# A hybrid decoder layer: the output projection as seven block products, its weights made ahead by jobs

## The chip, the cores and the metric

The kernel runs on one core of a Trainium2 chip. The time is the device time of one execution in microseconds, from three runs. The engines are TensorE (PE, matrix products), VectorE (DVE), ScalarE (ACT), GpSimd (POOL) and SyncE (SP), which here issues transfers. Transfers run on the core's 16 DMA engines.

## The reference

One layer on 1024 positions of width 1024, float32. What matters here:

```python
merged = (gates[:, :, 0] * (y_a @ w_branch_a[l])
          + gates[:, :, 1] * (y_b @ w_branch_b[l])
          + gates[:, :, 2] * (y_c @ w_branch_c[l]))
x = x + merged @ w_out[l]
x = x + 0.5 * swiglu(rmsnorm(x, ffn2_norm[l]), ffn2_w_gu[l], ffn2_w_down[l])
```

Ahead of it stand a first such FFN (`ffn1`, d_ff 2816) and the three branches a (spatial gating), b (latent attention) and c (memory attention). The change concerns the product of `y_b`, the gates' middle term, the product with `w_out`, and where their weights are prepared.

## The kernel before

**Arithmetic.** Float32 products are made of three: every operand is split into a high part (an ACT copy to a rounded type, tiles `whi`) and a low part (a DVE subtraction, `wlo`), `split` at L139 and L142 (or L146 and L147). `mm3` (L158 to L160) issues high x high, high x low and low x high into one PSUM bank, as 128x128 weights against 128x512 columns. Activations lie transposed: 8 tiles of 128 features, and two halves of 512 positions each.

**Fewer products in the FFNs.** The FFNs already multiply 2 x 2 blocks with seven products instead of eight. Their operands are sums of blocks named `b11`, `b12`, `b22`, `b21`, `t1` to `t4`: for activations made by `OpNorm` out of the normalised rows, for weights by `sums` (L1443) and stored or kept as splits.

**The first FFN's down** (`down`, from L2088) is a nest of seven loops, one for each product, with six steps each: five with 24 matmuls and one with 12. `fetch` (L2117) has SP load the quarter blocks of w_down (L2126, only in the first three loops) and a slice of the stored activations (`tdb..`, `tdt..`, L2128). `ahead()` calls it three steps ahead of use, and `prepare` (L2137) splits what came, one step ahead. Extra work hangs on steps (loop, step): `pre` in front of the matmuls, `post` behind them. There `gates.first(0)` (transfers of four blocks) stands at (1, 0), `gates.sums(0)` (four DVE sums, L1443) at (1, 4), and `norm.tokens(0)`, whose PE transposes are L410 and whose DVE reduction is L413, ahead of the matmuls of (5, 2). PE, SP, DVE and ACT run this in the order in which the code is written; a transfer that SP must wait for holds all behind it.

**The middle branch** (`branch_pairs(1, ...)`) takes 16 steps of 12 matmuls. DVE multiplies each with its gate (L573), GpSimd adds what the other two branches left in `mc` (L574), and the sum is split into `merged`.

**The projection** (`project`, L1146) runs over two halves and eight column tiles; each loads a 128x1024 tile of `w_out`, splits it, and makes 8 x 3 matmuls into a bank, which DVE adds to the rows of `x` (L1155), read back from `x1d`. `norm.feed` squares them on ACT and sums the squares on DVE (L1302, L1307). With half 0 done, the tasks `norm.first()` (sums and root, turn, part 0, part 1) are spread over the first four columns of half 1: DVE reduces (L413), takes the root (L192, then from L169 to L185), PE broadcasts (L425), DVE multiplies (L1344) and makes blocks (L1367, L147). PE reaches the units of the second FFN, which use these blocks, behind half 1; behind the first nine matmuls there stand half 1's token sums (L394).

Three tiles `raw` of 512 KB (128x1024, one tag with three buffers) serve loads of weights that are to be split.

## Time and profile before

| what | before |
|---|---|
| time, median of 3 runs | 2162.37 us (2161.65 to 2163.86) |
| the profiled execution | 2163.03 us |
| its span, first to last instruction | 2161.3 us |
| mean granted TensorE clock | 0.999 |

The time is that of the whole execution, the span that of the instructions in the trace. In the rows of groups and of the timeline, an entry names line, engine, operation, output and inputs; "x8" is a count. In the rows of windows, busy microseconds stand for each engine with their counts, then the clock, the share of the DMA engines and GB/s. Rows of transfers give KB of one and the median time from issue to landing.

### The profile page before, as it was taken

What the parts mean: (1) busy time and instruction counts of PE and PEld (TensorE: products, weight loads), DVE (VectorE), ACT (ScalarE), POOL (GpSimd) and SP (SyncE); (2) the same over time, 40 slices, a digit from 0 to 9 for tenths busy, and PEclk for the clock granted to TensorE, in tenths of its full rate; (3) what the DMA queues carried; (4) which work ended last, traced back from release to release, by engine and by line L of the source; (5) the groups of instructions that cost most, each with busy time, mean ns of one, the idle gap of its engine ahead of it and who ended that gap; (6) DMA issues with size and microseconds to landing.
All of it is one profiled execution on the core that took longest, in us unless ns stands there. A gap on an engine that the chain in (4) does not pass through costs nothing.

```text
span 2161.3 us, 27448 instructions
## 1 busy us (share of the span) xinstructions
PE 2151.9 (100%) x10112; PEld 1797.8 (83%) x10112; DVE 1572.1 (73%) x2371; ACT 910.3 (42%) x1486; POOL 255.0 (12%) x256
## 2 busy tenths in 40 slices
PE   9999999999999999999999999999999999999999
PEld 6888888888887888888988889988888888888887
DVE  7966666679889657655786679886876666657884
ACT  6433333243455434433555378833433223224332
POOL 0011111100000000000123311240011212110000
PEclk9999999999999999999999999999999999999999
DMA  4264555385332445641587832293133332347443
GB/s 148 92 220 159 190 180 175 119 318 193 118 124 94 147 164 180 223 149 61 212 283 259 314 105 69 75 348 104 40 127 103 110 97 100 103 144 288 169 129 104
DMA packets 137175, 342.56 MB, mean 158 GB/s; under 512 B 21713, under 2 KB 30033, under 8 KB 137041
## 3 DMA queue, kind: packets, MB, share of 16 engines
q1 hardware_dynamic: 136896, 340.81, 45.9%
q8 instruction: 79, 1.29, 0.2%
q14 instruction: 56, 0.45, 0.1%
q10 hardware_dynamic: 144, 0.00, 0.0%
HBM read 230.90 MB, written 109.86 MB: 158 GB/s over the span
## 4 chain that ended last, share of the span: by engine, by line
PE 91%; DVE 6%; ACT 1%; DMA 1%; issue 1%; SPq 0%; POOL 0%; ACTq 0%; DVEq 0%; POOLq 0%
PE one L158 15%; PE one L159 15%; PE one L160 15%; PE bank L158 13%; PE bank L159 13%; PE bank L160 13%; PE mm L158 1%; PE mm L159 1%; PE mm L160 1%; PE bank L1019 1%; PE one L1967 1%; DVE w L147 1%; DVE wlo L147 1%; DVE pr L997 1%; DVE wlo L142 1%
## 5 line engine op out<-in xcount | busy, mean ns | idle before, releaser
L146 ACT CAST whi<-x 128x1024 fp32r<-128x1024 f32 x202 | 192.3, 955 | 414.4 <-DVE x L1443 170.4
L147 DVE TENSOR_TENSOR wlo<-x,whi 128x1024 fp32r<-128x1024 f32 x202 | 241.2, 1195 | 58.9 <-ACT whi L146 19.6
L1471 DVE TENSOR_TENSOR t<-t,one 128x512 f32<-128x512 f32 x188 | 128.9, 686 | 190.8 <-PE one L160 190.7
L158 PE MATMUL bank<-h,whi 128*128 128x512 f32 x636 | 247.9, 390 | 0.0
L160 PE MATMUL bank<-h,wlo 128*128 128x512 f32 x636 | 247.5, 389 | 0.0
L159 PE MATMUL bank<-h,whi 128*128 128x512 f32 x636 | 247.5, 389 | 0.0
L158 PE MATMUL one<-h,whi 128*128 128x512 f32 x508 | 199.0, 392 | 0.0
L159 PE MATMUL one<-h,whi 128*128 128x512 f32 x508 | 198.4, 390 | 0.0
L160 PE MATMUL one<-h,wlo 128*128 128x512 f32 x508 | 198.3, 390 | 0.0
L158 PE MATMUL one<-w,whi 128*128 128x512 f32 x432 | 168.5, 390 | 0.0
L159 PE MATMUL one<-w,whi 128*128 128x512 f32 x432 | 168.1, 389 | 0.0
L160 PE MATMUL one<-w,wlo 128*128 128x512 f32 x432 | 168.1, 389 | 0.0
L142 DVE TENSOR_TENSOR wlo<-w,whi 128x1024 fp32r<-128x1024 f32 (+2 forms) x112 | 114.4, 1036 | 67.3 <-ACT whi L139 67.1
L139 ACT CAST whi<-w 128x1024 fp32r<-128x1024 f32 (+2 forms) x112 | 98.8, 901 | 149.8 <-PE one L159 55.6
L2067 POOL TENSOR_TENSOR raw<-raw 128x512 f32<-128x512 f32 x38 | 57.0, 1499 | 794.8 <-DVE raw L1908 684.8
L160 PEld LDWEIGHTS bank<-h,wlo 128*128 128x128 f32 x636 | 119.4, 188 | 24.9
L159 PEld LDWEIGHTS bank<-h,whi 128*128 128x128 f32 x636 | 119.4, 188 | 24.6
L158 PEld LDWEIGHTS bank<-h,whi 128*128 128x128 f32 x636 | 119.4, 188 | 24.4
L158 PE MATMUL bank<-whi 128*128 128x512 f32 x352 | 136.9, 389 | 0.0
L159 PE MATMUL bank<-wlo,whi 128*128 128x512 f32 x352 | 136.9, 389 | 0.0
L160 PE MATMUL bank<-whi,wlo 128*128 128x512 f32 x352 | 136.9, 389 | 0.0
L160 PEld LDWEIGHTS one<-h,wlo 128*128 128x128 f32 x508 | 95.8, 189 | 20.1
(406 smaller groups left out, 4892.2 us busy)
## 6 DMA issues: line engine op xcount, KB each, us to landing
x<-in_ffn_w_gu_dram SPq DMA_DIRECT2D x78, 512.0 KB, 5.1
w<-tdt SPq DMA_DIRECT2D x40, 512.0 KB, 4.2
gate<-raw SPq DMA_DIRECT2D x33, 512.0 KB, 3.0
tdb<-raw SPq DMA_DIRECT2D x64, 256.0 KB, 2.1
h<-in_ffn_w_down_dram SPq DMA_DIRECT2D x64, 256.0 KB, 6.0
w<-tdb SPq DMA_DIRECT2D x30, 512.0 KB, 5.1
tdt<-w SPq DMA_DIRECT2D x48, 256.0 KB, 2.4
x<-in_w_gate_dram SPq DMA_DIRECT2D x22, 512.0 KB, 5.9
```

The lines of the kernel that those rows point to most:

```text
L139: i = self.nc.scalar.copy(hi, src)
L142: return (eng or self.nc.vector).tensor_tensor(lo, src, hi.bitcast(F32), op=ALU.subtract)
L146: self.nc.scalar.copy(hi, src)
L147: return lambda: self.nc.vector.tensor_tensor(lo, src, hi.bitcast(F32), op=ALU.subtract)
L158: i = mmul(out, s[0], m[0], start=first, stop=False, **kw)
L159: mmul(out, s[0], m[1], start=False, stop=False, **kw)
L160: self.last = mmul(out, s[1], m[0], start=False, stop=last, **kw)
L997: nc.vector.tensor_tensor_reduce(out=pr[:, :m], in0=sc[:, :m], in1=self.mask[:, m0:m0 + m], scale=1.0, scalar=-NEG, op0=ALU.add, op1=ALU.m ...
L1019: nc.tensor.transpose(b[:, at:at + P], prs[t][:, kk * P:(kk + 1) * P], self.ident)
L1471: return self.nc.vector.tensor_tensor(out, x, y, op=ALU.add)
L1967: k.last = nc.tensor.matmul(b, w, norm.x(half, c), start=c == 0, stop=c == DT - 1)
L2067: sub = lambda d, x, y: (eng or nc.gpsimd).tensor_tensor(d, x, y, op=ALU.subtract)
```

## The change

The projection becomes seven products of 2 x 2 blocks, as in the FFNs (`merge`). Each has 4 column tiles x 4 row tiles x 3 matmuls. Its weights (`wo`, as high and low parts for each of seven products and two groups of columns) are made ahead: three of the fourteen by the existing jobs in `ffn1`'s up, eleven by `out_jobs` in `ffn1`'s down. Such a job loads 512 KB of `w_out` (or of a stored sum) into a `raw` tile, has GpSimd issue a transfer that adds a second block into it where two blocks make the sum (eight of eleven jobs), four steps later stores the sum where another job needs it (four of them), and a step after that splits the tile and stores both parts. Job i starts at step 4 + 7i // 4 of the 42, counted through the loops.

The middle branch is made in block order (b11, b12, b22, b21); in place of GpSimd's additions, eight transfers issued from GpSimd add `mc` into its tiles. DVE makes the sums of blocks and splits. The halves are swapped: what was half 0 of the rows is now half 1, in loads of `x1d` and in the stores. Norm and first weights of the second FFN are made within `merge`: the sum of squares is complete with the fifth product (for half 0), `norm.sums` stands at the second quarter of the sixth, `turn` and the first part behind its last, the second part behind the first quarter of the seventh. `gates.first` goes to step (4, 4) of the down loops, `gates.sums` to (5, 1). `layout` stores `w_out` as four quadrants.

The diff without the small parts (a bank argument of `turned_sums` and `norm_scale`, `store`'s columns, `layout`):

```diff
+        self.wo = self.dram.tile([7, 2, 2, P, D], F32, name="wo")
+        wo = [self.rounded(self.a["w_out"][g, i].unsqueeze(1), self.wo[n, g]) for n, i, g in ((0, 0, 0), (0, 0, 1), (6, 2, 0))]
         when = {}
-        for first, some in ((0, jobs), (1, small)):
+        for first, step, some in ((0, 2, jobs), (1, 2, small), (13, 2, wo[:2]), (16, 1, wo[2:])):
             for n, job in enumerate(some):
                 for f in range(2):
-                    at = when.setdefault(first + 2 * n + f, [])
+                    at = when.setdefault(first + step * n + f, [])
                     at.insert(0 if f else len(at), lambda job=job: next(job))
...
-        merged = [self.hrows() for _ in range(2)]
-        for _ in self.branch_pairs(
-                1, yb, mc, None, each, lambda d, f, x: self.split(*merged[f][d], x)):
-            pass
-        return merged
-
-    def project(self, merged, norm, sink):
...
+        return yb, mc
+    def out_jobs(self):
+        sums = self.dram.tile([3, 2, P, D], F32, name="wosum")
+        A11, A12, A22, A21 = range(4)
+        w, sync = self.a["w_out"], self.nc.sync
+        parts = {4: ((A11,), A21, 0), 1: (0, A22, 1), 3: (1, A12, None), 2: ((A21,), A22, None),
+                 0: ((A11,), None, None), 5: ((A12,), None, None), 6: ((A22,), None, None)}
+        def job(n, g):
+            x, (first, more, put) = self.raw(), parts[n]
+            sync.dma_start(x, sums[first, g] if isinstance(first, int) else w[g, first[0]])
+            if more is not None:
+                self.nc.gpsimd.dma_start(x, w[g, more], accum_op=ALU.add)
+            yield
+            if put is not None:
+                sync.dma_start(sums[put, g], x)
+            yield
+            hi, lo = self.wide("whi"), x.bitcast(F32R)
+            self.split(hi, lo, x)
+            for d, t in zip(self.wo[n, g], (hi, lo)):
+                sync.dma_start(d, t.bitcast(F32))
+            yield
+        order = [(n, g) for n in (4, 2, 1, 5, 3) for g in range(2)] + [(6, 1)]
+        when = {}
+        for i, j in enumerate(order):
+            j, q = job(*j), 4 + i * 7 // 4
+            for at, k in ((q, 2), (q + 4, 1), (q + 5, 0)):
+                when.setdefault(at, []).append((k, j))
+        return {(q // 6, q % 6): [lambda j=j: next(j) for _, j in sorted(x, key=lambda y: y[0])] for q, x in when.items()}
+    def merge(self, yb, mc, room, norm, load, early, later, sink):
+        nc, tt, h4 = self.nc, self.nc.vector.tensor_tensor, self.h4
+        names = ("b11", "b12", "b22", "b21")
+        raw = {n: [room() for _ in range(2)] for n in names}
+        w, op, x, banks = {}, {}, norm.x, {}
+        def put(name, p, src):
+            hi, lo = h4(F32R), h4(F32R)
+            op.setdefault(name, {})[p] = (hi, lo)
+            self.split(hi, lo, src)
+        def branch(name, k):
+            top, col = name[1] == "2", name[2] == "2"
+            dt, hf = 4 * top + k, int(col)
+            if dt not in w:
+                y = self.load(self.a["w_branch"][1, dt // 2])
+                w[dt], w[dt + 1] = y[:4], y[4:]
+            sig, d = self.row(), raw[name][k // 2]
+            nc.sync.dma_start(sig, self.sig[DT + dt][:, hf])
+            b = self.bank()
+            self.branch(b, w[dt], yb, hf)
+            tt(d[:, k % 2], sig, b, op=ALU.mult)
+            if k % 2:
+                nc.gpsimd.dma_start(d, mc[dt - 1:dt + 1, :, hf].rearrange("k p t -> p k t"), accum_op=ALU.add)
+        def weights(n):
+            out = []
+            for g in range(2):
+                ts = self.wide("whi"), self.wide("wlo")
+                for t, src in zip(ts, self.wo[n, g]):
+                    nc.sync.dma_start(t.bitcast(F32), src)
+                out += [tuple(t[:, u * 512:u * 512 + 512] for t in ts) for u in range(2)]
+            return out
+        def product(key, take, ws, name, first, last=True):
+            if first:
+                banks[key] = [None] * 4
+            for u in range(4):
+                if first:
+                    banks[key][u] = take()
+                for k in range(4):
+                    m = tuple(t[:, k % 2] for t in op[name][k // 2])
+                    s = tuple(t[:, k * P:(k + 1) * P] for t in ws[u])
+                    self.mm3(banks[key][u], s, m, first and k == 0, k == 3, skip_group_check=True)
+                yield u, banks[key][u]
+        def add(half, c, b, sign=ALU.add, parts=1):
+            y = x(half, c)
+            for n in self.parts(parts):
+                tt(y[:, n], y[:, n], b[:, n], op=sign)
+        for k in range(4):
+            branch("b11", k)
+            if k % 2:
+                put("b11", k // 2, raw["b11"][k // 2])
+        for k in range(4):
+            branch("b12", k)
+        ws = weights(0)
+        for k in range(4):
+            branch("b22", k)
+            if k % 2:
+                p = k // 2
+                b11, b12, b22 = (raw[n][p] for n in ("b11", "b12", "b22"))
+                tt(b12, b12, b22, op=ALU.subtract)
+                tt(b11, b12, b11, op=ALU.subtract)
+                put("t2", p, b11)
+        for k in range(4):
+            branch("b21", k)
+        load()
+        w2 = weights(1)
+        for u, b in product("a", self.single, ws, "b11", True):
+            add(1, 2 * u + 1, b, ALU.subtract)
+        p1 = banks["a"]
+        for p in range(2):
+            b11, b22 = raw["b11"][p], raw["b22"][p]
+            put("b22", p, b22)
+            nc.vector.scalar_tensor_tensor(b22, in0=b22, scalar=-1.0, in1=b11, op0=ALU.mult, op1=ALU.subtract)
+        for p in range(2):
+            put("t1", p, raw["b22"][p])
+        ws = weights(2)
+        for u, b in product("x", self.bank, w2, "t2", True):
+            add(1, 2 * u + 1, b, ALU.subtract)
+        for u in range(4):
+            add(0, 2 * u, p1[u])
+        for p in range(2):
+            put("t3", p, raw["b12"][p])
+        w2 = weights(3)
+        for u, b in product("x", None, ws, "t1", False):
+            add(0, 2 * u + 1, b, ALU.subtract)
+        for u in range(4):
+            add(0, 2 * u + 1, p1[u], ALU.subtract)
+        early()
+        for p in range(2):
+            put("b21", p, raw["b21"][p])
+            tt(raw["b21"][p], raw["b21"][p], raw["b11"][p], op=ALU.add)
+        ws = weights(4)
+        for u, b in product("x", None, w2, "b22", False):
+            add(0, 2 * u, b)
+            norm.feed(0, 2 * u)
+        for p in range(2):
+            put("t4", p, raw["b21"][p])
+        w2 = weights(5)
+        for u, b in product("y", self.bank, ws, "t3", True):
+            add(0, 2 * u + 1, b)
+            norm.feed(0, 2 * u + 1)
+            sink(0, 2 * u + 1)
+        ws = weights(6)
+        later()
+        norm.take = self.single
+        for u, b in product("a", None, w2, "b21", False):
+            add(1, 2 * u, b)
+            if u == 1:
+                with self.tc.high_priority(offset=600):
+                    norm.sums(0)
+            elif u == 3:
+                norm.turn(0)
+                norm.take = None
+                norm.part(0)
+            norm.feed(1, 2 * u)
+        for u, b in product("y", None, ws, "t4", False):
+            parts = 2 if u == 3 else 1
+            if u == 0:
+                norm.part(1)
+            add(1, 2 * u + 1, b, parts=parts)
+            norm.feed(1, 2 * u + 1, parts)
+            sink(1, 2 * u + 1)
 
...
-                    {(1, 0): [do(gates.first, 0)], (1, 4): [do(gates.sums, 0)],
+                    {(4, 4): [do(gates.first, 0)], (5, 1): [do(gates.sums, 0)],
...
-                    late)
+                    late, self.out_jobs())
...
-            merged = self.mixer(latents)
+            yb, mc = self.mixer(latents)
...
-            for half in range(2):
-                for p in range(DT // 2):
-                    nc.sync.dma_start(rows.take(half, p), x1d[half, p])
             norm = OpNorm(self, rows, lambda: self.g_ffn2)
             ffn = SwiGLU(self, a["ffn2_w_gu"], a["ffn2_w_down"], fp, norm, 2)
-            for f in range(2):
-                ffn.fetch(f, [ffn.w4] * 4)
-            self.project(merged, norm, lambda half, c: keep(x2d, norm.t, half, c))
+
+            def load():
+                for half, p in ((1, 0), (1, 1), (1, 2), (1, 3), (0, 0), (0, 1), (0, 2), (0, 3)):
+                    nc.sync.dma_start(rows.take(half, p), x1d[1 - half, p])
+
+            def early():
+                for f in range(2):
+                    ffn.fetch(f, [ffn.w4] * 4)
+
+            made = {}
+
+            def later():
+                for f in range(2):
+                    ffn.sums(f)
+                    made[f] = ffn.weights(f, "t")
+
+            with tc.manual_schedule(engines={mybir.EngineType.PE}):
+                self.merge(yb, mc, ffn.w4, norm, load, early, later, lambda half, c: keep(x2d, norm.t, half, c))
...
-                for act in [*acts[n, s], *post.get((n, s), ())]:
+                for act in [*acts[n, s], *post.get((n, s), ()), *jobs.get((n, s), ())]:
```

**SP in the first FFN's down.** Rows of SP while loop 1 (counted from 0) runs and slices for loop 2 (`tdt1_1`) are fetched. `in_ffn1_w_down_dram` is w_down, `in_x_dram` the residual input, a number behind a name tells tiles apart. Before:

```order
L2126 DMA w4_3663<-in_ffn1_w_down_dram 128x512
L2126 DMA w4_3665<-in_ffn1_w_down_dram 128x512
L2128 DMA w4_3949<-tdt1_1_99 128x1024
L1180 DMA x4_3951<-in_x_dram 128x2x512
L2126 DMA w4_3730<-in_ffn1_w_down_dram 128x512
L2126 DMA w4_3732<-in_ffn1_w_down_dram 128x512
L2128 DMA w4_3996<-tdt1_1_99 128x1024
L1180 DMA x4_3998<-in_x_dram 128x2x512
```

And now:

```order
L1154 DMA raw_3977<-wosum_3392 128x1024
L2281 DMA w4_3692<-in_ffn1_w_down_dram 128x512
L2281 DMA w4_3694<-in_ffn1_w_down_dram 128x512
L2283 DMA w4_3989<-tdt1_1_99 128x1024
L1323 DMA x4_3991<-in_x_dram 128x2x512
L1164 DMA wo_794<-whi_4031 128x1024
L1164 DMA wo_794<-raw_3799 128x1024
L1154 DMA raw_4036<-wosum_3392 128x1024
L2281 DMA w4_3753<-in_ffn1_w_down_dram 128x512
L2281 DMA w4_3755<-in_ffn1_w_down_dram 128x512
L2283 DMA w4_4044<-tdt1_1_99 128x1024
L1323 DMA x4_4046<-in_x_dram 128x2x512
```

Between the fetches there now stand the stores of a job's two parts (L1164) and, right behind them, the load of a later job (L1154) into one of the three `raw` tiles.

**DVE ahead of half 0's transposes in loop 5.** `L1307` of before and `L1462` now are the sums of squares, `L413` is the reduction behind the transposes (PE, L410 before). Before:

```order
L142 TENSOR_TENSOR wlo_4741<-h4_3640,whi_4740 128x512
L142 TENSOR_TENSOR wlo_4741<-w4_3642,whi_4740 128x512
L142 TENSOR_TENSOR wlo_4747<-w4_4647,whi_4746 128x1024
L2195 SCALAR_TENSOR_TENSOR x4_3925<-bank_4432,x4_3925 128x512
L1307 TENSOR_TENSOR t_4471<-t_4471,t_4711 128x512
L1307 TENSOR_TENSOR t_4471<-t_4471,t_4751 128x512
L413 TENSOR_REDUCE ts_4758<-bank_4759 128x4
```

And now:

```order
L142 TENSOR_TENSOR wlo_4855<-w4_4755,whi_4854 128x1024
L2350 SCALAR_TENSOR_TENSOR x4_3962<-bank_4524,x4_3962 128x512
L1462 TENSOR_TENSOR t_4563<-t_4563,t_4819 128x512
L1598 TENSOR_TENSOR x4_4752<-raw_4749,raw_4750 128x512
L1598 TENSOR_TENSOR raw_4751<-raw_4750,x4_4752 128x512
L1598 TENSOR_TENSOR x4_4752<-raw_4749,raw_4751 128x512
L1598 TENSOR_TENSOR raw_4751<-raw_4750 128x512
L1462 TENSOR_TENSOR t_4563<-t_4563,t_4859 128x512
L413 TENSOR_REDUCE ts_4870<-bank_4871 128x4
```

The four sums of `gates.sums` (L1598, L1443 of before) have moved between the last two sums of squares.

**DVE at the start of the second FFN.** From the last of the norm's multiplies (L1344 before, L1499 now) on. L147 with an `h4` output is the low part of a block for the units, first of `b22`, then of `t3`; L1367 (now L1522) makes `t3`, L1155 (now L1229) adds a bank to the rows. Before:

```order
L1344 SCALAR_TENSOR_TENSOR x4_12874<-x4_12874,c_ffn2_norm_3304,bank_13300 128x512 x2
L142 TENSOR_TENSOR wlo_13484<-raw_13481,whi_13483 128x512 x2
L1307 TENSOR_TENSOR t_13240<-t_13240,t_13296 128x512
L147 TENSOR_TENSOR h4_13348<-x4_12876,h4_13347 128x1024
L1367 TENSOR_TENSOR x4_12872<-x4_12876,x4_12872 128x1024
L1155 TENSOR_TENSOR x4_12882<-x4_12882,bank_13313 128x512
L1367 TENSOR_TENSOR x4_12874<-x4_12878,x4_12874 128x1024
L142 TENSOR_TENSOR wlo_13521<-raw_13518,whi_13520 128x512 x2
L1155 TENSOR_TENSOR x4_12882<-x4_12882,bank_13363 128x512
L147 TENSOR_TENSOR h4_13352<-x4_12872,h4_13351 128x1024
```

And now:

```order
L1499 SCALAR_TENSOR_TENSOR x4_12959<-x4_12959,c_ffn2_norm_3326,one_13472 128x512 x2
L147 TENSOR_TENSOR wlo_13599<-w4_13187,whi_13598 128x1024
L1462 TENSOR_TENSOR t_13405<-t_13405,t_13490 128x512
L147 TENSOR_TENSOR h4_13483<-x4_12961,h4_13482 128x1024
L1229 TENSOR_TENSOR x4_12949<-x4_12949,bank_13296 128x512
L1522 TENSOR_TENSOR x4_12957<-x4_12961,x4_12957 128x1024
L1229 TENSOR_TENSOR x4_12951<-x4_12951,bank_13314 128x512
L1522 TENSOR_TENSOR x4_12959<-x4_12963,x4_12959 128x1024
L1229 TENSOR_TENSOR x4_12953<-x4_12953,bank_13332 128x512
L1462 TENSOR_TENSOR t_13405<-t_13405,t_13519 128x512
L1229 TENSOR_TENSOR x4_12955<-x4_12955,bank_13350 128x256 x2
L147 TENSOR_TENSOR h4_13487<-x4_12957,h4_13486 128x1024
```

In both pieces the last row is the low part of `t3`'s first tiles. Between the multiplies and that row there now stand four additions of the seventh product's banks (the last in two parts) and two sums of squares, the splits of `w_out` (L142, `raw`) are gone.

38 lines of the change are left out of this document (11 added, 27 removed).

## The prediction

> **What bounds the kernel now.** First the page's rows of the span, of busy time and of the transfer rate by slice (a slice is 54 us), then three rows of the waits of TensorE (PE):
>
> ```profile
> span 2161.3 us, 27448 instructions
> PE 2151.9 (100%) x10112; PEld 1797.8 (83%) x10112; DVE 1572.1 (73%) x2371; ACT 910.3 (42%) x1486; POOL 255.0 (12%) x256
> GB/s 148 92 220 159 190 180 175 119 318 193 118 124 94 147 164 180 223 149 61 212 283 259 314 105 69 75 348 104 40 127 103 110 97 100 103 144 288 169 129 104
> ...
> PE bank L231 <- POOL ident masks.py:199: 1.5, 1, 1.5
> PE one L158 <- DVE raw L1471: 0.7, 2, 0.5
> PE bank L425 <- DVE rs_y L185: 0.7, 1, 0.7
> ```
>
> PE is one unbroken stream: its largest wait, for the identity matrix at the start, is 1.5 us, the next are under one. So two things change the time: matmuls added or taken away, and any new wait of PE. Work of the other engines, GpSimd (POOL) too, counts only where PE comes to wait for it. The profiled execution took 2163.0 us (1.7 lie outside its span), 0.7 over the median of 2162.37; I work from 2163.0.
>
> **The gain: matmuls.** PE's timeline, and the window of 80 us inside the old projection (PE busy and its count come first, DMA share and GB/s last):
>
> ```profile
> 1524.81 0.39 PE L158 MATMUL bank<-h,whi 128*128 128x512 f32 x1
> 1525.04 0.39 PE L159 MATMUL bank<-h,whi 128*128 128x512 f32 x1
> 1525.27 0.39 PE L160 MATMUL bank<-h,wlo 128*128 128x512 f32 x1
> ...
> 1445.00:1525.00 80.00, 80.00 (x358) 66.26 (x357) 51.01 (x81) 28.76 (x45) 0.00 (x0) 1.00 0.37 138
> ```
>
> A record lasts 0.39 us, yet the next one starts 0.23 later: records overlap, and the price of a matmul is the distance between starts. Eight of the 358 are transposes of 128 columns, some 0.7 us together, so a full one costs (80 - 0.7) / 350 = 0.2266 us. The old projection had 2 x 8 x 8 x 3 = 384, the seven products have 7 x 4 x 4 x 3 = 336, the middle branch keeps its 192. Saved: 48 x 0.2266 = **10.9 us** (with 0.39 it would be 18.7, too much). One product is 10.9 us as well, a quarter of it 2.72.
>
> **Cost 1: the start of the second FFN.** Rows of the timelines of VectorE (DVE) and PE there before:
>
> ```profile
> 1488.61 0.68 DVE L413 TENSOR_REDUCE ts<-bank 128x4 f32<-128x512 f32 x1
> ...
> 1490.41 0.16 DVE L192 TENSOR_SCALAR rms_v<-ts 128x4 f32<-128x4 f32 x1
> 1490.61 0.17 DVE L169 TENSOR_SCALAR rs_y<-rms_v 128x4 int32<-128x4 int32 x1
> ...
> 1494.54 5.35 DVE L1344 SCALAR_TENSOR_TENSOR x<-x,c_ffn_norm,bank 128x512 f32<-128x512 f32 x8
> 1499.80 1.29 DVE L142 TENSOR_TENSOR wlo<-raw,whi 128x512 fp32r<-128x512 f32 x2
> ...
> 1502.74 1.22 DVE L1367 TENSOR_TENSOR x<-x,x 128x1024 f32<-128x1024 f32 x1
> 1503.88 0.68 DVE L1155 TENSOR_TENSOR x<-x,bank 128x512 f32<-128x512 f32 x1
> 1504.48 1.22 DVE L1367 TENSOR_TENSOR x<-x,x 128x1024 f32<-128x1024 f32 x1
> ...
> 1521.61 0.69 DVE L1155 TENSOR_TENSOR x<-x,bank 128x512 f32<-128x512 f32 x1 [1.28 <-PE bank L160]
> ...
> 1526.85 0.39 PE L158 MATMUL one<-h,whi 128*128 128x512 f32 x1
> 1527.05 0.75 DVE L1155 TENSOR_TENSOR x<-x,bank 128x256 f32<-128x256 f32 x2 [3.31 <-PE bank L160]
> ...
> 1528.89 0.50 PE L394 MATMUL bank<-ones,t 128*128 128x1 f32 x4
> ```
>
> Prices from start to start: 0.60 us for 128x512, 1.14 for 128x1024, 0.20 for a tiny one of the root, 5.3 for the eight multiplies of the norm. Half 0's norm began at 1488.6 and the units that use it at 1526.85: 38 us, in which DVE even ran idle (the row at 1521.61). After the change half 0 is complete only with the fifth product, and two products, 21.8 us, lie between that and the units. Let T be the first matmul of the sixth. From the order of the changed kernel, DVE has from T up to the low part of t3's first tiles, with which the units begin: 13 additions and sums of squares (7.8 us), two of half width (0.7 by the row at 1527.05), the reduction (0.6), nine tiny ones (1.8), the eight multiplies (5.3), seven of 128x1024 (8.0), together 24.2, and some 2.6 idle before the reduction, as its transposes stand behind the sixth product's second quarter: T + 26.8. Behind it come two of 128x1024, two of 128x512 and the two halves of the last sum of squares, 4.2 us, for which the token sums (L394) wait: T + 31.0. PE without waits is at the units at T + 21.8 + 0.7 (the same eight small ones as in the window above) = T + 22.5, and at the token sums nine matmuls (2.0 us) later, T + 24.5. So PE loses 31.0 - 24.5 = **6.5 us**, 4.3 of them at the units' first matmul, the rest between there and the token sums. From the token sums on the order is as before.
>
> **Cost 2: the eleven jobs in the first FFN's down.** Windows of before over that loop nest (PE, PEld, DVE, ACT, POOL busy, clock, DMA share, GB/s), the busiest short window that I found for the DMA engines, and landings (last number) of the nearest transfers:
>
> ```profile
> 432.00:462.00 30.00, 30.00 (x134) 24.86 (x133) 24.66 (x31) 11.58 (x17) 5.14 (x3) 1.00 0.88 319
> 462.00:492.00 30.00, 30.00 (x135) 24.82 (x134) 21.44 (x36) 13.44 (x21) 0.00 (x0) 1.00 0.88 314
> 492.00:522.00 30.00, 30.00 (x134) 24.86 (x133) 28.40 (x53) 10.58 (x15) 0.00 (x0) 1.00 0.62 217
> 522.00:552.00 30.00, 30.00 (x134) 24.86 (x133) 29.45 (x55) 12.96 (x21) 0.00 (x0) 1.00 0.39 112
> 552.00:582.00 30.00, 30.00 (x134) 24.82 (x134) 25.34 (x37) 13.18 (x20) 0.00 (x0) 1.00 0.38 118
> ...
> 1399.90:1401.00 1.10, 1.10 (x7) 0.90 (x6) 0.55 (x1) 0.62 (x1) 0.00 (x1) 1.00 1.02 371
> ...
> raw<-in_w_out_dram SPq DMA_DIRECT2D x16, 512.0 KB, 4.0
> gate<-raw SPq DMA_DIRECT2D x33, 512.0 KB, 3.0
> w<-tdt SPq DMA_DIRECT2D x40, 512.0 KB, 4.2
> x<-x1d SPq DMA_DIRECT2D x8, 512.0 KB, 7.5
> ```
>
> The jobs add 11 loads, 8 accumulating transfers, 4 stores of sums and 22 stores of weights, 45 x 0.524 = 23.6 MB between about 457 and 575 us. Against the page's best slice, 348 GB/s, before leaves room for 1.2 MB until 492 (5 us at 29 GB/s, 30 at 34), 3.9 MB until 522, 7.1 until 552, 6.9 until 582. By the jobs' steps 14 transfers (7.3 MB) fall before 492, 14 (7.3) before 522, 11 (5.8) before 552, six (3.1) after: the backlog is 6.1, then **9.5**, 8.2 and 4.4 MB. 9.5 MB is 27 us at 348 GB/s. SP issues in written order, and each fourth and later load waits for the landing of the stores from the same raw tile: three tiles, a new job every 1.75 steps (some 9 us), a tile held for five steps, a split and a store, over 30 us. Behind such a load stand the weight fetches, which are issued three steps (3 x 24 matmuls, 16 us) ahead. So PE would wait about 27 - 16 = **11 us**. At 371 GB/s the room is 1.5 MB more, the backlog 22 us, the wait 5.
>
> The Trainium skill, "DMA: Bandwidth & Descriptors", "Where 436 GB/s comes from", names 435 GB/s as the limit on the SBUF side and some 358 where HBM (the chip's memory) binds. The rows agree with the lower one so far (348 over a slice, 371 over a microsecond). By 358 my estimate of the wait is 9 us; by 435 the backlog would be 3.9 MB, 9 us of transfers, and the wait nothing, which is rival 2.
>
> An accumulating transfer stands in no row. If it costs one plain load, 4.0 us, the sum holds; if it also reads its destination, a load and a store, 7.0, then the six of them before 522 add 6 x 0.524 = 3.1 MB, 9 us more. I know nothing for a price below a plain load. I take one load, the nearest row. In the middle branch the eight of them have over 10 us each until their sums are read, so that either price is hidden there.
>
> The Trainium skill, same page, "Anatomy of one DMA — SWDGE (gpsimd) path", has 2.0 us and 436 KB per us for a transfer issued from GpSimd: by my estimate 3.2 us for 512 KB, with which the sum would stay as it is.
>
> DVE gets eleven more subtracts of 128x1024, 12.5 us, between 482 and 570, where its idle time is 2.9 + 1.6 + 0.6 + 2.8 = 7.8 us by the windows: about **5 us** late even if no transfer were. I count these 5 inside the 11, since a PE that waits for transfers gives DVE the time.
>
> **Cost 3: gates.sums just ahead of half 0's transposes.** DVE's last row before them, then PE's:
>
> ```profile
> 598.87 1.48 DVE L1307 TENSOR_TENSOR t<-t 128x512 f32<-128x512 f32 x2
> ...
> 601.47 0.60 PE L410 MATMUL bank<-ident,t 128*128 128x128 f32 x4
> ```
>
> DVE ended at 600.35, PE came at 601.47: 1.1 us of slack. Four sums of 0.60 now stand ahead of the last of these additions: 2.4 - 1.1 = 1.3 us at least, 3.4 with another 128x1024 subtract and the slack already used up; I take **2**.
>
> **At nothing.** Without GpSimd's additions PE wins nothing: it waited for none of them. gates.first only moves fetches later, to where the windows show a DMA share of 0.38. The reloads of x1d go out behind weights of the merge; if one lands late (7.5 us by its row, less the quarter of 2.72 ahead of the addition), PE loses up to 4.8 us. I take nothing, because the first addition to these rows comes only after the sixteen steps of the middle branch have been issued, and keep 4.8 for the range. The sums of blocks between the products fit: DVE was busy 51 of 80 us in the old projection, and up to the fourth product no norm waits on it.
>
> **Sum:** -10.9 + 6.5 + 11 + 2 = +8.6; 2163.0 + 8.6 = **2171.6 us**. With costs 2 and 3 and x1d at their ends (the wait for transfers 5 to 20, gates.sums 1.3 to 3.4, x1d 0 to 4.8) it is 2164.9 to 2186.8.
>
> **Rivals.**
>
> 1. Faster: fetches pass through. Much of the backlog is stores that are read only in the merge, hundreds of microseconds later. If a raw tile is free by the time that its next load is issued, SP is not held, the fetches get their share of the engines, and DVE's subtracts fall into gaps: costs 2 and 3 go, and -10.9 + 6.5 = -4.4, 2158.6. It turns when a tile is held for less than three job distances, 27 us. For it: the share of 0.39 from 522 on. Against: 0.88 until 492 and DVE's 29.45 of 30. Its best end, with the norm chain hidden as well, is 2152.1.
> 2. Only DVE is late: -10.9 + 6.5 + 5 + 2 = +2.6, 2165.6. It needs the backlog at 522 to stay under 16 us, and solving 14.7 MB less the room against 16 us gives 398 GB/s as its point. Against it: the highest row is 371.
> 3. Accumulating transfers are dear: 9 us more, 2180.6, and with x1d late 2185. A tile is then also held longer. The Trainium skill's page "SBUF — State Buffer" ("Who interferes with whom") has some DVE instructions and GpSimd exclude each other at a shared port, so that a transfer issued from GpSimd may wait for DVE; no run here shows such a transfer yet.
> 4. The change does not do what it says, so that the 48 matmuls stay: excluded, the changed program has 48 fewer.
>
> **How the numbers follow.** The forecast (2168 to 2178) has 0.40, rival 1 0.22, rival 2 0.18, rival 3 0.20. A measurement of this kernel tells about 0.2% (4.3 us) from no change: the bounds are 2158.1 and 2166.7. Rival 1 lies just above the first, so I give 0.15 to faster and the rest of it to no difference, with most of rival 2: 0.21; slower 0.64. The range must leave out at most 0.2: the best end of rival 1 (0.08) and what is above rival 3 with everything (0.10): **2156 to 2188**.
>
> **What would show it.** The matmuls: 48 records fewer, starts still 0.2266 apart. Cost 1: in the waits, PE idle some 4 us for a low part of t3 at the second FFN's first unit and 2 at the token sums. Cost 2: PE idle for weight splits (whi or wlo) between 470 and 590, with SP's rows of loads late and a DMA share near 0.9 to beyond 522; if PE waits there while the share stays low, SP's order alone did it. Cost 3: PE idle for a sum of squares ahead of the transposes in the loop of index 5. I am wrong if PE's waits sum to under 11 us, then the change is faster; or if a new wait stands in the merge, which I hold to be free.

## The result, and the profile after

The changed kernel takes 2211.16 us (median of 6 runs, 2207.85 to 2213.23), the kernel before on the same chip 2163.11 (6 runs, 2161.65 to 2164.94): a ratio of 1.0221, 95% interval [1.0208, 1.0234]. It is 48 us slower. The forecast was 2171.6 with a range to 2188, so the sign was right and the size far off.

From the page of the changed kernel (the profiled execution took 2207.85 us): the span, the busy times, the granted clock by slice, and the two queues of transfers that matter (packets, MB, share of 16 engines).

```profile
span 2205.8 us, 27424 instructions
PE 2163.5 (98%) x10064; PEld 1798.8 (82%) x10064; DVE 1582.3 (72%) x2379; ACT 911.2 (41%) x1466; POOL 246.2 (11%) x256
...
PEclk9999999998999999999999999999999999999999
...
q1 hardware_dynamic: 143520, 367.03, 48.1%
q0 software_dynamic: 3328, 8.39, 2.1%
```

There are 48 matmuls fewer (10064 against 10112), as the change says. But PE is no longer at 100%, and one digit of the clock's row has fallen to 8, where all were 9 before. The waits of PE in the changed kernel, the largest first (total, times, longest):

```profile
PE bank L158 <- ACT whi L139: 8.9, 4, 5.2
PE bank L158 <- DVE w L1201: 5.9, 1, 5.9
PE one L158 <- ACT whi L139: 5.5, 2, 4.1
PE one L159 <- DVE h L147: 3.1, 1, 3.1
PE bank L159 <- DVE wlo L142: 3.1, 5, 0.8
PE bank L410 <- DVE t L1462: 3.0, 1, 3.0
PE bank L158 <- issue: 2.1, 1, 2.1
```

They belong to three places. Rows with L139, with `wlo` and with L410 lie in the first FFN's down; L1201 and "issue" in the merge; L147 at the start of the second FFN. How much each place lost is read best from windows, by counting matmuls. The down, first of before, then of the changed kernel:

```profile
490.00:650.00 160.00, 160.00 (x711) 132.51 (x710) 144.59 (x232) 71.95 (x107) 0.00 (x0) 1.00 0.43 139
```

```profile
490.00:650.00 160.00, 138.27 (x545) 108.79 (x544) 121.53 (x198) 63.09 (x92) 4.34 (x5) 0.90 0.77 255
1465.00:1515.00 50.00, 41.97 (x166) 33.63 (x165) 31.87 (x38) 10.12 (x10) 4.84 (x4) 0.90 0.92 295
```

In 160 us before made 711 matmuls, 0.225 us each; the changed kernel made 545. The missing 166 are **37.4 us**. PE stood idle for only 160 - 138.27 = 21.7 of them. The other 15.7 went while PE was at work: the granted clock in that window is 0.90. In the merge (second row) 50 us hold 166 matmuls in place of 50 / 0.2266 = 221: **12.4 us**, 8.0 of them idle. At the start of the second FFN it is 6.0 us (below). The sum is -10.9 + 37.4 + 12.4 + 6.0 = +44.9, and the spans differ by 2205.8 - 2161.3 = 44.5: the four terms account for the difference to within half a microsecond.

**Why a wait costs more than its length.** PE's timeline behind one wait in the down, then the window around it:

```profile
534.60 0.80 PE L158 MATMUL bank<-whi 128*128 128x512 f32 x1 [5.18 <-ACT whi L139]
535.86 0.79 PE L159 MATMUL bank<-wlo,whi 128*128 128x512 f32 x1 [0.46 <-DVE wlo L142]
536.45 0.63 PE L160 MATMUL bank<-whi,wlo 128*128 128x512 f32 x1
536.88 0.63 PE L158 MATMUL bank<-whi 128*128 128x512 f32 x1
537.30 0.63 PE L159 MATMUL bank<-wlo,whi 128*128 128x512 f32 x1
...
534.00:537.00 3.00, 1.94 (x4) 1.24 (x5) 2.42 (x4) 0.55 (x1) 0.00 (x0) 0.50 1.05 272
```

Behind the wait starts are 0.43 us apart, not 0.23, at a granted clock of 0.50. Behind a shorter wait, at 514.6 us, this lasted until 521.5. The Trainium skill says it in "TensorE: Matmul & The Clock Gate", "What's actually happening": after some 3.4 us of idling the array gets half its clock, and the full one back after as long at work. The trace agrees in kind; here the waits were shorter, 2.2 us before the matmul at 514.6 and 0.5 behind it. Length alone does not decide it: at L410 PE waits 2.96 us in the changed kernel and 2.96 in e7 (below); starts 0.43 us apart follow in the first, none in the second. The trace before has such a stretch only at its very beginning, from 39.6 to 42.6 us at a granted clock of 0.51, and there not behind a wait but behind 24 matmuls of one column each.

**What holds SP.** SP's timeline in the same stretch of the changed kernel, and the largest of its own waits between 440 and 660 us:

```profile
513.17 0.41 SPq L1164 DMA_DIRECT2D wo<-whi  x1
513.68 0.40 SPq L1164 DMA_DIRECT2D wo<-raw  x1
526.01 0.32 SPq L1154 DMA_DIRECT2D raw<-wosum  x1
526.38 0.90 SPq L2281 DMA_DIRECT2D w<-in_ffn_w_down_dram  x2
527.33 0.43 SPq L2283 DMA_DIRECT2D w<-tdt  x1
...
SPq L1154 <- DMA wo<-raw: 57.5, 8, 11.3
SPq L1164 <- ACT whi L139: 18.9, 5, 5.8
```

A job's store goes out at 513.7; the load behind it needs the same raw tile and waits for the store's landing, until 526.0. For 12 us nothing is issued, and behind it stand the blocks of w_down and the slice that the next steps split. Eight such loads waited 57.5 us.

The engines were not full all that time. Between 522 and 552 us, where PE made 73 matmuls in place of 134:

```profile
522.00:552.00 30.00, 19.84 (x73) 14.97 (x72) 14.54 (x25) 8.56 (x12) 0.86 (x1) 0.83 0.77 236
```

A share of 0.77 and 236 GB/s leave room, which points to SP's order by the sign that the prediction had named, PE waiting while the share is low. Before 522 the share was 1.05 (462 to 492) and 0.96 (492 to 522), so the engines had their part too.

### The profile page after: what moved, and what is told of

It is laid out like the page before. It is cut to its first block, busy times and chain, and to the rows that moved or that the text cites. A ratio compares the mean times of both kernels' runs of the same rounds, so it can differ in the third digit from the quotient of the medians.

```text
span 2205.8 us, 27424 instructions
## 1 busy us (share of the span) xinstructions
PE 2163.5 (98%) x10064; PEld 1798.8 (82%) x10064; DVE 1582.3 (72%) x2379; ACT 911.2 (41%) x1466; POOL 246.2 (11%) x256
## 3 DMA queue, kind: packets, MB, share of 16 engines
q1 hardware_dynamic: 143520, 367.03, 48.1%
q0 software_dynamic: 3328, 8.39, 2.1%
## 4 chain that ended last, share of the span: by engine, by line
PE 84%; DVE 8%; DMA 4%; issue 2%; ACT 1%; SPq 0%; POOL 0%; DVEq 0%; ACTq 0%; POOLq 0%
PE one L158 15%; PE one L159 14%; PE one L160 14%; PE bank L158 11%; PE bank L159 11%; PE bank L160 10%; DVE wlo L142 1%; PE mm L158 1%; PE mm L159 1%; PE mm L160 1%; DMA wo<-raw 1%; DMA w<-tdt 1%; PE bank L1021 1%; DVE pr L999 1%; PE one L2122 1%
## 5 line engine op out<-in xcount | busy, mean ns | idle before, releaser
L147 DVE TENSOR_TENSOR wlo<-x,whi 128x1024 fp32r<-128x1024 f32 x202 | 238.8, 1183 | 68.7 <-DMA wkv<-wlo 24.3
L158 PE MATMUL bank<-h,whi 128*128 128x512 f32 x588 | 230.0, 391 | 2.1 <-issue 2.1
L159 PE MATMUL bank<-h,whi 128*128 128x512 f32 x588 | 229.5, 390 | 0.0
L160 PE MATMUL bank<-h,wlo 128*128 128x512 f32 x588 | 229.4, 390 | 0.0
L159 PE MATMUL one<-h,whi 128*128 128x512 f32 x540 | 211.0, 391 | 3.3 <-DVE h L147 3.1
L158 PE MATMUL one<-h,whi 128*128 128x512 f32 x540 | 211.8, 392 | 0.2 <-ACT h L146 0.2
L160 PE MATMUL one<-h,wlo 128*128 128x512 f32 x540 | 210.7, 390 | 0.0
L142 DVE TENSOR_TENSOR wlo<-w,whi 128x1024 fp32r<-128x1024 f32 (+2 forms) x112 | 114.4, 1037 | 84.3 <-ACT whi L139 84.1
L139 ACT CAST whi<-w 128x1024 fp32r<-128x1024 f32 (+2 forms) x112 | 98.6, 901 | 164.9 <-PE one L159 58.3
L158 PEld LDWEIGHTS bank<-h,whi 128*128 128x128 f32 x588 | 110.7, 188 | 25.3 <-issue 2.5
L160 PEld LDWEIGHTS bank<-h,wlo 128*128 128x128 f32 x588 | 110.8, 188 | 23.2
L159 PEld LDWEIGHTS bank<-h,whi 128*128 128x128 f32 x588 | 110.8, 188 | 22.8
L159 PEld LDWEIGHTS one<-h,whi 128*128 128x128 f32 x540 | 101.8, 188 | 25.4 <-DVE h L147 4.3
```

The lines of the kernel that those rows point to most:

```text
L139: i = self.nc.scalar.copy(hi, src)
L142: return (eng or self.nc.vector).tensor_tensor(lo, src, hi.bitcast(F32), op=ALU.subtract)
L147: return lambda: self.nc.vector.tensor_tensor(lo, src, hi.bitcast(F32), op=ALU.subtract)
L158: i = mmul(out, s[0], m[0], start=first, stop=False, **kw)
L159: mmul(out, s[0], m[1], start=False, stop=False, **kw)
L160: self.last = mmul(out, s[1], m[0], start=False, stop=last, **kw)
```

## Experiments

Two theories of the down: **A**, SP's written order with three raw tiles; **B**, the traffic, with an accumulating transfer at twice its bytes. A third candidate is DVE. Loss in the down means, below, the matmuls missing between 490 and 650 us against 711, times 0.225 us.

**e2: no jobs.**

```diff
-                    late, self.out_jobs())
+                    late)
...
-                for t, src in zip(ts, self.wo[n, g]):
+                for t, src in zip(ts, self.wo[0, g]):
```

> The eleven jobs are left out and every product takes the weights of the first product, so the output is not the reference's; the merge and its transfers stay. Theories A and B both expect the loss between 490 and 640 us (38 us by the counts of matmuls) to go, except some 4 us at the transposes of half 0, which come from the place of the four sums: 2172 to 2178. If more is lost elsewhere than I read, it stays above 2185.

Measured: 2177.44 us (2174.14 to 2179.51). The same window of its trace, and PE's wait at half 0's transposes:

```profile
490.00:650.00 160.00, 158.76 (x704) 131.18 (x704) 143.14 (x232) 71.73 (x107) 0.00 (x0) 1.00 0.45 147
...
PE bank L410 <- DVE t L1462: 1.2, 1, 1.2
```

704 matmuls: 1.6 us are lost, so the jobs cost nearly all of the 37. The 1.6 are the place of the four sums by itself (cost 3), less than the 4 that were expected. What is left, 14.6 us more than before, is for the most part merge and second FFN less the saving; the merge alone loses nearly 15 us in this trace (156 matmuls in the 50 us from 1430).

**e1: the jobs' loads issued by GpSimd.**

```diff
-            sync.dma_start(x, sums[first, g] if isinstance(first, int) else w[g, first[0]])
+            self.nc.gpsimd.dma_start(x, sums[first, g] if isinstance(first, int) else w[g, first[0]])
```

> The loads of the jobs in the first FFN's down (L1154) are issued by GpSimd, no longer by SP; traffic, DVE work and stores stay. Theory A (SP's written order: a load that waits for the stores of its raw tile holds the weight fetches behind it, 57.5 us of such waits in the changed kernel) expects most of the loss of the down to go: 2180 to 2195 us against 2211, and no wait of SP at L1154. Theory B (the DMA engines are full, accumulating transfers count double) expects little: 2204 to 2211.

Measured: 2195.05 us (2194.35 to 2197.78), 16 us less, at the upper edge of what A expected. The window of its trace, and the queue of GpSimd's transfers from its page:

```profile
490.00:650.00 160.00, 145.72 (x613) 116.86 (x612) 137.64 (x220) 71.72 (x103) 8.76 (x13) 0.96 0.79 270
...
q0 software_dynamic: 4912, 14.16, 2.9%
```

The loss in the down fell from 37.4 to 22.1 us with the bytes unchanged; it is now GpSimd that waits for the raw tiles, and SP goes on. The queue took 0.8% more for the 5.77 MB of plain loads, 0.139% per MB, while the accumulating transfers cost it 0.250% (below): it is the adding that is dear, not this queue.

**e6: the raw tile held a step less.**

```diff
-            for at, k in ((q, 2), (q + 4, 1), (q + 5, 0)):
+            for at, k in ((q, 2), (q + 3, 1), (q + 4, 0)):
```

> The jobs split and store one step earlier (four steps behind the load, not five), so a raw tile is held about 5 us less; loads stay on SP, traffic is the same. Theory A (SP is held by loads that wait for a raw tile): SP's waits at L1154 fall from 57 us to under 30 and the time to 2190 to 2200. Theory B (full DMA engines): 2206 to 2213.

Measured: 2196.34 us (2194.18 to 2197.88), as A expected. SP's wait at L1154 fell from 57.5 to 16.4 us:

```profile
SPq L1154 <- DMA wo<-raw: 16.4, 4, 7.3
```

Two different edits that free SP give 15 to 16 us.

**e3: no accumulating transfers in the jobs.**

```diff
-            if more is not None:
-                self.nc.gpsimd.dma_start(x, w[g, more], accum_op=ALU.add)
```

> The eight accumulating transfers of the jobs are left out (the sums lack their second block, so the output is not the reference's), everything else of the jobs stays. Theory B, with a double price for an accumulating transfer, frees 16 of 53 units of traffic: 2190 to 2200. Theory A expects the same holds of SP, since each load still waits for the stores ahead of it: 2203 to 2211, SP's waits at L1154 over 45 us.

Measured: 2195.99 us (2188.41 to 2200.07), as B expected. But SP's wait at L1154 fell too:

```profile
SPq L1154 <- DMA wo<-raw: 31.0, 8, 8.0
```

A store of a part landed after 3.3 us (median) in place of 6.5, where the engines had less to do. A and B are not two separate shares, one feeds the other.

**e7: e1, and the stores a step behind the split.**

```diff
             self.split(hi, lo, x)
+            yield
             for d, t in zip(self.wo[n, g], (hi, lo)):
...
-            for at, k in ((q, 2), (q + 4, 1), (q + 5, 0)):
+            for at, k in ((q, 2), (q + 4, 1), (q + 5, 0), (q + 6, -1)):
```

> As e1 (loads issued by GpSimd, 2195 us), and the stores of the parts (L1164) a step behind their split, so that SP no longer waits for ACT and DVE there (44 us of such waits in e1). If SP's order makes up what e1 left: 2182 to 2190. If it is the full DMA engines (388 GB/s at a share of 1.03 from 480 to 510 us in e1): 2192 to 2198.

Measured: 2190.14 us (2184.58 to 2194.44): between the two expectations, and its runs scatter too much to say more. In its trace, of an execution of 2184.58 us, the loss in the down is 18.7 us.

**e11: e7 and e3 together.**

> e7 and e3 together: the jobs' loads on GpSimd, stores a step later, and no accumulating transfer in the jobs (the sums lack their second block, the output is not the reference's). If SP's order and the dear transfers are the whole loss of the down, it comes to e2, which has no jobs: 2177 to 2181. What is left above that is DVE's and ACT's extra work or the plain traffic: 2182 to 2190.

Measured: 2187.04 us (2183.80 to 2195.39): not down to e2. 642 matmuls in the window of its trace (of an execution of 2195.39 us) leave 15.5 us lost; even its shortest run is 4 us above the longest of e2. So a third share stands beside A and B.

**e13 and e14: no subtracts by the jobs**, first in the changed kernel, then in e11.

```diff
-            self.split(hi, lo, x)
+            self.nc.scalar.copy(hi, x)
```

> The eleven jobs make no low part on DVE (the raw tile itself is stored in its place, so the output is not the reference's); transfers and their order stay. If DVE's 12.5 us of subtracts are a loss beside the transfers: 2195 to 2203. If they hide behind the waits for transfers, as the prediction counted them: 2206 to 2212.

> e11 without DVE's subtracts of the jobs (and without accumulating transfers; the output is not the reference's): loads, stores and casts remain. If the 13 us that e11 still loses between 500 and 650 us are DVE's, they fall to under 5: 2177 to 2181. If they are the plain traffic: 2185 to 2190.

Measured: 2201.70 us (2198.82 to 2203.61) for e13, 9 less than the changed kernel and as expected if the subtracts are a loss beside the transfers; 2182.37 (2178.32 to 2186.36) for e14, between its two expectations. The window of e14:

```profile
490.00:650.00 160.00, 154.84 (x671) 125.44 (x670) 135.18 (x220) 79.82 (x115) 4.23 (x8) 0.99 0.71 250
```

671 matmuls, 9.0 us lost, against 15.5 in e11: the subtracts are some 6.5 us of it by these two traces, 4.7 by the medians of runs that overlap, about what the prediction had for them alone (5). That they do not hide behind the waits for transfers, e13 shows best: 9 us less, although SP's wait at L1154 stays (60.8 us). Of the last 9 us some 4 are at the transposes, and the rest was not divided further.

**e8: gates.sums behind step (5, 4).**

```diff
-                    {(4, 4): [do(gates.first, 0)], (5, 1): [do(gates.sums, 0)],
-                     (5, 3): [do(norm.high, 0), do(norm.low, 0)], (5, 4): [do(norm.apart, 0), do(gates.first, 1)],
+                    {(4, 4): [do(gates.first, 0)],
+                     (5, 3): [do(norm.high, 0), do(norm.low, 0)], (5, 4): [do(norm.apart, 0), do(gates.first, 1), do(gates.sums, 0)],
```

> gates.sums stands behind step (5, 4) rather than (5, 1), out of the way of half 0's transposes; nothing else. Cost 3 as predicted, with the slow restart behind it: PE's wait of 3 us there goes and the time falls by 4 to 6, to 2205 to 2207. If only the sums were moved into another stretch that is full: 2209 to 2213.

Measured: 2210.58 us (2204.61 to 2215.11), no gain that these runs can show. PE's waits in its trace say why:

```profile
PE bank L394 <- DVE t L1462: 2.0, 2, 1.8
...
PE bank L410 <- DVE t L1462: 0.5, 1, 0.5
```

The wait at L410 fell from 3.0 to 0.5 us, and one of 1.8 came at the token sums behind the loops. The four sums were moved out of one full stretch into another.

**e4 and e5: the merge, DVE's order.** In the changed kernel DVE reaches the first difference of blocks and waits there, while the next multiply, which would free PE's bank, stands behind it. DVE, then PE:

```profile
1461.46 0.69 DVE L1201 TENSOR_TENSOR w<-t,bank 128x512 f32<-128x512 f32 x1 [1.37 <-PE bank L160]
1476.34 1.23 DVE L1243 TENSOR_TENSOR w<-w,w 128x1024 f32<-128x1024 f32 x1 [14.19 <-DMA w<-mc]
1477.48 0.68 DVE L1201 TENSOR_TENSOR w<-t,bank 128x512 f32<-128x512 f32 x1
...
1478.22 0.80 PE L158 MATMUL bank<-x,whi 128*128 128x512 f32 x1 [5.92 <-DVE w L1201]
```

e4 writes the differences behind the last multiply:

```diff
             branch("b22", k)
-            if k % 2:
-                p = k // 2
...
         for k in range(4):
             branch("b21", k)
+        for p in range(2):
+            b11, b12, b22 = (raw[n][p] for n in ("b11", "b12", "b22"))
+            tt(b12, b12, b22, op=ALU.subtract)
...
```

> In the merge the sums of blocks b12 - b22 and what follows are written behind the last step of the middle branch, so that DVE frees the banks of b21 before it waits for the accumulating transfers. If DVE's wait in its order is what held PE at 1478 us (5.9 us idle and the slow restart), 2200 to 2204; if PE merely waits for the same transfers at its first product of t2 instead, 2209 to 2213.

Measured: 2210.63 us (2207.37 to 2213.59). The scheduler kept DVE's order as it was, so this run tells nothing of either theory. e5 adds a dependency that forces it:

```diff
-            tt(d[:, k % 2], sig, b, op=ALU.mult)
+            op["last"] = tt(d[:, k % 2], sig, b, op=ALU.mult)
...
-            tt(b12, b12, b22, op=ALU.subtract)
+            self.after(tt(b12, b12, b22, op=ALU.subtract), op["last"])
```

> As e4, whose DVE order had not changed; now the first difference of blocks is also tied behind the last multiply of the middle branch, so DVE frees all banks before it waits for an accumulating transfer. Theory DVE order: PE's 7 us wait for DVE's multiply in the merge and its slow restart go: 2197 to 2203 us. Theory GpSimd: accumulating transfers are issued only every 6 us, the sums come too late anyway and PE waits as long at the product of t2: 2207 to 2213.

Measured: 2208.64 us (2205.01 to 2210.33), within the second expectation. GpSimd's timeline in e5, with the landing time of the first of the two transfers, and PE's largest wait:

```profile
1471.91 1.20 POOL L1203 DMA_DIRECT2D w<-mc  x1 [4.72 <-issue]
...
DMA to landing us min/median/max: 11.3/11.3/11.3
...
1483.50 1.22 POOL L1203 DMA_DIRECT2D w<-mc  x1 [10.39 <-issue]
...
PE bank L158 <- ACT h L139: 8.6, 1, 8.6
```

The banks come free now, and PE waits for the blocks of t2 instead, longer than before. DVE's order was not the cause. A transfer issued at 1471.9 landed at 1483.2, and the next was issued 0.3 us later, though its data had been ready: the accumulating transfers ran one at a time. DVE did not hold GpSimd back there either: in the changed kernel DVE is idle from 1462.2 to 1476.3 (rows above), and in that time too the transfer at 1468.31 went out only 0.3 us behind the landing of the one before.

**e9: accumulating transfers of 256 KB.**

```diff
-            if k % 2:
-                nc.gpsimd.dma_start(d, mc[dt - 1:dt + 1, :, hf].rearrange("k p t -> p k t"), accum_op=ALU.add)
+            nc.gpsimd.dma_start(d[:, k % 2], mc[dt][:, hf], accum_op=ALU.add)
```

> In the merge each accumulating transfer is cut in two of 256 KB, issued behind its own multiply (16 in all). In the trace each 512 KB one began within 0.4 us of the landing of the one before. If what keeps them apart is room for their rows (256 rows of 2 KB each; halves have 128, like those of the jobs, which do overlap), they overlap now and the sums come early: 2197 to 2204 us. If each simply waits for the one before, 16 landings of some 4 us take longer than the 44 us of the branch: 2209 to 2220.

Measured: 2200.76 us (2200.47 to 2202.32), as expected of transfers that overlap. GpSimd's timeline in e9:

```profile
1442.20 2.71 POOL L1202 DMA_DIRECT2D w<-mc  x3 [3.67 <-DVE w L1201]
```

Three go out back to back. A limit in bytes does not explain it, since in the down two of 512 KB, with 128 rows of 4 KB each, are in flight together. GpSimd's timeline there in the changed kernel, and the landing times of the eight:

```profile
465.31 1.07 POOL L1156 DMA_DIRECT2D raw<-in_w_out_dram  x1 [14.33 <-DMA w<-in_ffn_w_down_dram]
469.61 0.86 POOL L1156 DMA_DIRECT2D raw<-in_w_out_dram  x1 [3.24 <-DMA raw<-in_w_out_dram]
...
DMA to landing us min/median/max: 7.8/8.9/9.9
```

With plain loads on the same queue there are up to three of 512 KB at once (e12). In no trace are more than three transfers of 128 rows in flight from GpSimd, 384 rows, and two of 256 never are. A limit on the rows in flight fits all of this; it was not tested by itself.

**e10: GpSimd's additions back in the middle branch.**

```diff
+            m = self.row()
+            nc.sync.dma_start(m, mc[dt][:, hf])
...
-            if k % 2:
-                nc.gpsimd.dma_start(d, mc[dt - 1:dt + 1, :, hf].rearrange("k p t -> p k t"), accum_op=ALU.add)
+            nc.gpsimd.tensor_tensor(d[:, k % 2], d[:, k % 2], m, op=ALU.add)
```

> The middle branch's accumulating transfers are undone: mc is loaded by SP and added by GpSimd as in the kernel before, everything else as changed. If the accumulating transfers cause the merge's loss (PE's 6 and 2 us and their slow restarts, 13 us by the matmuls' starts), 2196 to 2201. If the reloads of x1d or of weights hold PE there too, 2204 to 2211.

Measured: 2195.77 us (2195.47 to 2196.78), just below the range. The window that held the merge's loss:

```profile
1455.00:1505.00 50.00, 50.00 (x222) 41.44 (x221) 42.03 (x46) 10.24 (x10) 13.94 (x8) 1.00 0.88 334
```

222 matmuls in 50 us: nothing is lost. The merge's whole 12.4 us came from the accumulating transfers in place of GpSimd's additions.

**e12 and e15: what helped, together.** e12 is e7 with split and stores a step earlier, and e10; e15 puts the jobs' subtracts on GpSimd besides.

```diff
-            for at, k in ((q, 2), (q + 4, 1), (q + 5, 0)):
+            for at, k in ((q, 2), (q + 3, 1), (q + 4, 0), (q + 5, -1)):
...
```

> A version that gives the reference's output with what helped: e7 with the split and the stores one step earlier, and GpSimd's additions in the middle branch (e10). If the parts add up (21 of e7, some 4 of the shorter hold, 13 of the merge): 2172 to 2178. If the full DMA engines of the down remain: 2179 to 2186. Neither beats the kernel before.

```diff
-            self.split(hi, lo, x)
+            self.split(hi, lo, x, self.nc.gpsimd)
```

> e12 with the jobs' subtracts on GpSimd, which idles in the down; the output is the reference's. If DVE is the rest of the down's loss: 2172 to 2178 against 2183. If it is the traffic with accumulating transfers: 2181 to 2187.

Measured: 2183.30 us (2182.64 to 2183.73) for e12, as expected if full DMA engines remain, and 2187.40 (2184.64 to 2191.09) for e15, just above its second expectation. In e12 the merge is free of loss, but the down still loses 23.9 us by its window (605 matmuls), with the engines at 405 GB/s and a share of 1.04 between 480 and 510 us. e15 was no better: GpSimd's queue, which also has the loads, waits there 42.9 us for stores and 39.1 for ACT. e12 is still 21 us slower than the kernel before, and none of the versions beats that.

## Why the prediction was wrong

**The saving: right.** 48 matmuls fewer at 0.2266 us; the three losses and -10.9 add up to the difference of the spans within half a microsecond.

**Cost 1, the second FFN's start: right, 6.5 predicted, 6.0 measured.** PE, then DVE of the changed kernel:

```profile
1564.88 0.39 PE L160 MATMUL bank<-h,wlo 128*128 128x512 f32 x1
1565.49 0.50 PE L158 MATMUL one<-h,whi 128*128 128x512 f32 x1 [0.22 <-ACT h L146]
1569.14 0.62 PE L159 MATMUL one<-h,whi 128*128 128x512 f32 x1 [3.14 <-DVE h L147]
...
1573.14 1.05 PE L394 MATMUL bank<-ones,t 128*128 128x1 f32 x8
...
1567.86 2.35 DVE L147 TENSOR_TENSOR h<-x,h 128x1024 fp32r<-128x1024 f32 x2
```

Without a wait PE would have been at L394 ten starts behind 1564.88, at 1567.15; it came at 1573.14. The low part of t3 that PE waits for is the first of DVE's two at 1567.86. The sum of DVE's rows held: the sixth product begins at 1542.19 (T), and that row ends at 1569.08, T + 26.9, where the prediction had 26.8. The second wait, at the token sums, hardly shows, because PE came there late by itself, after a slow restart (starts 0.43 us apart from 1569.1 on). It would have been there: DVE was done with the first part of the last sum of squares only at 1573.09, with the second at 1573.42, T + 31.2, against 31.0.

**Cost 2, the jobs: the step that failed.** The prediction had 27 us of backlog less 16 us of fetching ahead, 11 us, with DVE's 5 inside. With cost 3 it came to 37.4. Three things were wrong in that step. First, SP's hold was named, and then left out of the sum: the 16 us of lead were counted as if SP kept issuing, but it stood still for up to 11.3 us at a time. The first tile was held for 39 us (457.0 to 495.8), as the "over 30" said and past the 27 at which rival 1 turns. Freeing SP gave 15 to 16 us (e1, e6). Second, an accumulating transfer was taken at one plain load. By the page's queues it has 2.1 / 8.39 = 0.250% of the engines per MB, a plain one 48.1 / 367.03 = 0.131%: 1.9 times as much. That was the prediction's upper bound and its rival 3. Leaving the eight out gave 15 us (e3); this is not to be set against the 9 of rival 3, which are the second half of the price for six of them, while e3 takes out the whole price of eight. Third, most of the longer stalls are followed by a stretch at half clock. PE lost 15.7 us in the down while it was at work, some 10 of them in 50 starts about 0.43 us apart, and the sum had no term for it. DVE's 5 us were somewhat small (9 in e13, 6.5 between e11 and e14), and they add to the others.

These shares overlap: e1, e3 and e13 alone give 16, 15 and 9 us, all three kinds of edit in e14 bring the down from 37.4 to 9.0 us. So a sum of separate prices cannot be made of them.

**Cost 3: right by itself.** 2 us predicted; without the jobs, in e2, the window loses 1.6, with 1.2 of waiting at L410. In the changed kernel PE waited 3.0 there and a slow stretch followed, 4.7 us by the starts. The excess comes with the jobs; by which of their parts was not divided. And e8 shows that moving the four sums wins nothing.

**"At nothing": wrong in the merge, 12.4 us.** "The eight of them have over 10 us each until their sums are read" took each transfer by itself. Their landing times in the changed kernel:

```profile
DMA to landing us min/median/max: 5.6/8.3/10.5
```

One goes out behind the other's landing, so that DVE waited 14 us for the fifth. A new wait in the merge was one of the two signs of being wrong that the prediction had named. The x1d loads, for which 4.8 us were kept, took no part: with them as they are, e10 loses nothing.

**The rate.** The 398 GB/s that rival 2 needed were reached: 405 GB/s over 30 us in e12 and e7. Of the two figures in the Trainium skill ("DMA: Bandwidth & Descriptors", "Where 436 GB/s comes from") the lower one, some 358 for HBM, did not bind here; the upper one, 435, was not exceeded. A higher rate did not save the kernel: at 405 GB/s the engines' share was 1.04, and PE waited all the same.

## What to carry to other kernels

Where the tensor engine never waits, a saving of matmuls has to be set against the first wait that the change brings, and where the clock drops behind it, that wait counts for 1.5 to 1.7 times its length (37.4 us lost for 21.7 idle, 12.4 for 8.0). A transfer queue that is issued in written order is a resource of its own: a load that reuses a tile behind its store holds all that stands behind it. An addition moved from an idle engine into the transfers isn't free: in the middle branch GpSimd's additions cost PE nothing (e10), and the accumulating transfers 12 us.

## What the runs showed of the hardware

An accumulating transfer took 1.9 times the DMA engines' time of a plain one per byte; its median landing was 8.9 us for 512 KB in the down and 8.3 in the merge. The jobs' plain loads of 512 KB in the same stretch of the down landed after 3.9 us when SP issued them, and after 6.8 when GpSimd did (e1). Those with 256 rows of 2 KB were never two at a time; those with 128 rows were, up to three. In the changed kernel matmuls of 128x512 started 0.43 us apart behind every wait of 2 us and more, for 3 to 7 us, at a granted clock of 0.50 (534 to 537 us); in other runs a wait of such a length could pass without it (2.96 us in e7, 3.34 in the merge of e2).
